# Low parts in two pieces, a later sums product, and a moved scaling in a float32 decoder kernel

## The chip, the cores and the metric

The kernel runs on one core of a Trainium2 chip. That core has TensorE for matrix products, VectorE and ScalarE for elementwise work, GpSimd (here it only issues DMAs), and SyncE, which issues most DMAs. The metric is the device time of one execution in microseconds. The profile names the engines PE (TensorE matmul), PEld (TensorE weight load), DVE (VectorE), ACT (ScalarE), POOL (GpSimd) and SP (SyncE). A line number such as L408 is a line of the kernel before the change.

## The reference

A decoder trunk of two layers works on one sequence of 512 tokens with 1024 features, all in float32. Each layer is half a SwiGLU FFN, a mixer, and half a second FFN, each behind an RMS norm. The first layer's mixer is a chunked gated linear attention (GLA), the second layer's a stick-breaking attention (SB). At the end stands one more RMS norm.

```python
def rmsnorm(x, g):
    xf = x.astype(jnp.float32)
    y = xf * lax.rsqrt(jnp.mean(xf * xf, axis=-1, keepdims=True) + EPS)
    return (y * g.astype(jnp.float32)).astype(x.dtype)

def swiglu(h, w_gate, w_up, w_down):
    return (jax.nn.silu(h @ w_gate) * (h @ w_up)) @ w_down
...
    for i in range(DEPTH):
        x = x + 0.5 * swiglu(rmsnorm(x, ffn1_norm[i]), ffn1_w_gate[i], ffn1_w_up[i], ffn1_w_down[i])
        h = rmsnorm(x, mix_norm[i])
        ...
        x = x + y.astype(x.dtype)
        x = x + 0.5 * swiglu(rmsnorm(x, ffn2_norm[i]), ffn2_w_gate[i], ffn2_w_up[i], ffn2_w_down[i])
    return rmsnorm(x, final_norm)
```

`w_gate` and `w_up` are 1024 x 2816, `w_down` is 2816 x 1024.

## The kernel before

**Number format.** Every operand of a product is cut into a high part (a cast to a reduced float32 on ScalarE, L148 for weights, tiles `wh`) and a low part (operand minus high part, a subtraction on VectorE, L150, tiles `wl`). A product of two operands is then three matmuls: high by high, low by high, high by low (`mm3`). Activations have the same two parts: `xh`/`xl` (not normed), `nh`/`nl` (normed), `hh`/`hl` (the FFN's inner values), `th`/`tl` (sums of normed halves).

**Phases.** Six phases follow one another: FFN, GLA, FFN, FFN, SB, FFN. The activations `xs` (eight tiles of 128 features by 512 tokens) stay on the chip. The weights stream in by DMA and are taken from one long list, `feed`; an entry is one or more weight tiles with a `body` that issues products and gives up control (`yield`) after pieces of them, so that other work can be put in between.

**An FFN phase.** Its first six entries work on activations that are not normed. Their results are multiplied by `R`, the inverse root of the mean square, when they leave the accumulator. `two_halves` runs the first two entries side by side: each has 24 matmuls and is driven in steps of six. In the three FFN phases after the first one (the third, fourth and sixth phase of all) a function is called in between: `sums_wide` adds up the squares over the features. ScalarE casts the sums to `sh` (L586), VectorE subtracts to `sl` (L588), and two matmuls with a matrix of ones go to the accumulator `ps_R`. `rstd_wide` makes `R` of it (L597 to L605, with a logarithm, an exponential and a square on ScalarE). Then `normed_input` (four pieces, L854 to L886) multiplies all eight `xs` by `R`, cuts them into `nh` and `nl`, and forms differences of their halves (`ts`). From the seventh entry on the products read `nh` and `nl`.

**Seven instead of eight products.** Larger blocks multiply two by two blocks with seven products and more additions (after Strassen and Winograd): `seven` for gate and up, `seven_down` for the down product of two of the six groups of inner features, two calls for each of those groups. So four FFNs have 16 `seven_down` in all. One `seven_down` consists of two entries with seven products of 12 matmuls (256 columns each) in this order: in `body_1` b11 (to accumulators `ws`, copied to `zs` by ScalarE), t1 (to `qs`), t2 (again to `ws`), b21 (to `zs`), and in `body_2` t3 (to `ws`), b22 (to `qs`), t4 (to `ws`). After each product `add` (L414, VectorE) takes the accumulator's content over into `xs`; the next product that goes to the same accumulator waits for that addition. `body_2` needs `s34`, two sums of weight blocks (VectorE, L399 and L400), cut into its parts by `split` at the end of the second step of `body_1`: the cast is ordered behind ScalarE's copies `v["copied"]`, the subtraction behind the last addition `added` of t1. Slice 0 to 1 of the parts is read by t3, slice 2 to 3 by b22.

**The end.** The last FFN ends token by token: `to_tokens` fetches the last norm's weights into `fin` (a DMA issued by GpSimd that gives all 128 partitions the same 1024 numbers), multiplies them by a constant on VectorE (L1617), and transposes `xs` on TensorE into `ps_T`, from which ScalarE copies them back (L1628). `back_tok` and `last` form the rest of the down product, the norm and the output.

**What sets the order.** A planner lays out each engine's instructions: it simulates the program with its own estimates and gives a free engine the ready instruction that stands first in the program. `tc.high_priority(n)` lets instructions count as n places earlier. `tc.issue_after(ins)`, also as `behind(ins)`, orders what is issued within it behind `ins`, for those instructions that run on the same engine as `ins`, without a wait for its end. Waits for data are put in by the framework, by the parts of a tile that are written and read. On the chip each engine runs its instructions strictly in the planned order.

Of the kernel before, what the change touches and what calls it, by code (L numbers as in the profile page):

```python
# [18 lines left out]
P = 128  # L19
T = 512  # L20
D = 1024
# [14 lines left out]
def flat(ps):  # L36

    return ps.rearrange("p (n two) -> p two n", two=2)
# [8 lines left out]
def decoder(ctx: ExitStack, tc: tile.TileContext, a: dict, out: bass.AP):  # L47
# [30 lines left out]

    def mm(ps, l, r, first, last):
        st["pe"] = nc.tensor.matmul(ps, l, r, start=first, stop=last).ins  # L80

    def mm3(ps, wh, wl, mh, ml, first, last):
        mm(ps, wh, turns(mh), first, False)
# [24 lines left out]
    def behind(ins):  # L108
        return tc.issue_after(ins) if ins is not None else ExitStack()

    class Entry:
# [13 lines left out]
                    self.views = [view(ch.load()) for ch, view, _, _ in self.units]  # L125
            return self.views

        def split(self, after=None, then=None):
            if self.W is None:
                self.W = []  # L130
                for r, (_, _, n, m) in zip(self.view(), self.units):
                    self.W.append(self.parts(r, n, m, after or self.casts_behind, then))

        def parts(self, r, n, m, after, then):
            few = n * m < 1024
            if few:

                h, l = (
                    st["few"].tile([P, n * m], F32R, tag="v" + t, bufs=1, name="w" + t) for t in "hl"
                )  # L140
            else:
                h, l = (wp.tile([P, n * m], F32R, tag="w" + t, bufs=4, name="w" + t) for t in "hl")
            h, l = (t.rearrange("p (n m) -> p n m", m=m) for t in (h, l))
            pieces = r if isinstance(r, tuple) else (r,)
            for i, part in enumerate(pieces):
                k = slice(i * n // len(pieces), (i + 1) * n // len(pieces))
                with behind(after):
                    nc.scalar.copy(h[:, k], part)  # L148
                with behind(then):
                    nc.vector.tensor_tensor(out=l[:, k], in0=part, in1=h[:, k].bitcast(F32), op=ALU.subtract)  # L150
            return h, l

    class Feed:
# [218 lines left out]
    def seven_down(pool, w, r0, hs, part):  # L372

        H = T // 2
        lower, upper = (
            Chunk(w[r0 : r0 + 4 * P, c : c + 256].rearrange("(f p) c -> p f c", p=P), 4, 256)
            for c in (part * 256, 512 + part * 256)
        )  # L380
        lower.few = upper.few = True
        v = {}

        def halves():

            lo, up = (c.load().rearrange("p (c two) d -> p two c d", two=2) for c in (lower, upper))
            return lo[:, 0], lo[:, 1], up[:, 0], up[:, 1]

        def sums_12(_):
            a11, _, a21, a22 = halves()  # L390
            s = v["s12"] = pool().tile([P, 4, 256], F32, tag="s", bufs=4, name="s12")
            nc.vector.tensor_tensor(out=s[:, 0:2], in0=a21, in1=a22, op=ALU.add)
            nc.vector.tensor_tensor(out=s[:, 2:4], in0=s[:, 0:2], in1=a11, op=ALU.subtract)
            return s

        def sums_34(_):
            a11, a12, a21, _ = halves()
            s = pool().tile([P, 4, 256], F32, tag="s", bufs=4, name="s34")
            nc.vector.tensor_tensor(out=s[:, 0:2], in0=a11, in1=a21, op=ALU.subtract)  # L399
            nc.vector.tensor_tensor(out=s[:, 2:4], in0=a12, in1=v["s12"][:, 2:4], op=ALU.subtract)  # L400
            return s

        def prod(ps, w, k0, m, b, first):
            for c in range(2):
                bh, bl = (turns(t) for t in hs[c][b])
                wh, wl = (t[:, k0 + c, m * P : (m + 1) * P] for t in w)
                for n, (l_, r_) in enumerate(((wh, bh), (wl, bh), (wh, bl))):
                    st["pe"] = nc.tensor.matmul(  # L408
                        ps, l_, r_, start=first and c + n == 0, stop=c == 1 and n == 2, skip_group_check=True
                    ).ins  # L410

        def add(m, up, col, ps):
            x = pair(xs[part * 2 + m + 4 * up][:, col * H : col * H + H])
            return nc.vector.scalar_tensor_tensor(out=x, in0=ps, scalar=0.5, in1=x, op0=ALU.mult, op1=ALU.add).ins  # L414

        def body_1(W):
            a11, s, v["a2"] = W
            ws, zs, qs = [], [], []
            for m in range(2):
                ws.append(psum("ps_w")[:, 0:H])  # L420
                prod(ws[m], a11, 0, m, "b11", True)
            for m in range(2):


                zs.append(psum("ps_z")[:, 0:H])
                with ahead():
                    v["copied"] = nc.scalar.copy(zs[m], ws[m]).ins
            yield

            ps = psum("ps_q")  # L430
            for m in range(2):
                qs.append(ps[:, m * H : (m + 1) * H])
                prod(qs[m], s, 0, m, "t1", m == 0)
            for m in range(2):
                added = add(m, 1, 1, flat(qs[m]))
            v["second"].split(v["copied"], added)
            yield
            for m in range(2):
                prod(ws[m], s, 2, m, "t2", False)
                add(m, 0, 1, flat(ws[m]))  # L440
            yield
            for m in range(2):
                prod(zs[m], v["a2"], 0, m, "b21", False)
                add(m, 0, 0, flat(zs[m]))
            v["w"], v["q"] = ws, qs
            yield

        def body_2(W):
            (s,) = W
            ws, qs = v["w"], v["q"]  # L450

            u3 = pool().tile([P, 2, H], F32, tag="c", bufs=1, name="u3")
            for m in range(2):
                prod(ws[m], s, 0, m, "t3", False)
                nc.scalar.copy(pair(u3[:, m]), flat(ws[m]))
                add(m, 1, 1, pair(u3[:, m]))
            yield
            for m in range(2):
                prod(qs[m], s, 2, m, "b22", False)
            for m in range(2):  # L460
                add(m, 0, 1, flat(qs[m]))
            yield
            for m in range(2):
                prod(ws[m], v["a2"], 2, m, "t4", False)
                add(m, 1, 0, flat(ws[m]))
            yield

        units = [(lower, lambda t: halves()[0], 2, 256), (lower, sums_12, 4, 256), (lower, lambda t: halves()[1::2], 4, 256)]
        feed.q.append(Entry(units, body_1))
        feed.q.append(Entry([(lower, sums_34, 4, 256)], body_2))  # L470
        v["second"] = feed.q[-1]
        feed.q[-1].v = v
# [106 lines left out]
        st["R"] = sp.tile([P, T], F32, tag="sq", name="R")  # L579
        nc.vector.tensor_copy(st["R"], ps)  # L580

    def sums_wide(pool):

        ss = st["ss"]
        h = sp.tile([P, T], F32R, tag="sq", name="sh")
        nc.scalar.copy(h, ss)  # L586
        l = pool.tile([P, T], F32R, tag="t", name="sl")
        nc.vector.tensor_tensor(out=l, in0=ss, in1=h.bitcast(F32), op=ALU.subtract)  # L588
        st["wide"] = ps = psum("ps_R")
        mm(ps, ones_r, turns(h), True, False)  # L590
        mm(ps, ones_r, turns(l), False, True)

    def rstd_wide():

# [12 lines left out]
    def two_halves(between=None):  # L607

        feed.finish()
        g = [feed.start(), feed.start()]  # L610
        for i in range(3):
            for x in g:
                next(x, None), next(x, None)
            if i == 0 and between is not None:
                between()

    def new_norm():
        st["h"], st["l"] = st["nh"], st["nl"]
# [16 lines left out]
    class FFN:  # L635
# [328 lines left out]
        def run(self, between=None):  # L964
            with tc.tile_pool(name="hp", bufs=8, reuse_waits="tile") as self.hp, tc.tile_pool(
# [4 lines left out]
                if st["ss"] is not None:  # L970
                    if self.after_ffn:
                        exp_ln_tables(st["closed"])
                    two_halves(lambda: sums_wide(self.tp))
                    rstd_wide()
                flush(self.defer)
                def spread(todo, n):
# [635 lines left out]
    def to_tokens(tp):  # L1612
        st["tp"] = tp
        fin = st["fin"] = tp.tile([P, D], F32, tag="s", bufs=4, name="fin")
        nc.gpsimd.dma_start(fin, a["final_norm"].partition_broadcast(P))

        nc.vector.tensor_scalar(out=fin, in0=fin, scalar1=2.0 * float(D) ** 0.5, scalar2=None, op0=ALU.mult)  # L1617

        for hf in range(2):
            ps = [psum("ps_T") for _ in range(NT)]  # L1620
            for m in range(4):
                for i in range(NT):
                    nc.tensor.transpose(
                        ps[i][:, m * P : (m + 1) * P], xs[hf * 4 + m][:, i * P : (i + 1) * P], ident
                    )
            for i in range(NT):
                xt[i, hf] = xs[hf * 4 + i]
                nc.scalar.copy(xt[i, hf], ps[i])  # L1628

    def last(dh, i, ps, c0, c1):  # L1630

# [335 lines left out]
```

## Time and profile before

| What | Value |
|---|---|
| median of 3 runs | 1772.12 us (1771.75 to 1773.25) |
| the profiled execution | 1772.11 us |
| its span in the trace | 1770.1 us |
| TensorE matmul busy | 1753.8 us (99%) |
| weight load busy | 1631.2 us (92%) |
| VectorE busy | 1505.5 us (85%) |
| ScalarE busy | 1062.8 us (60%) |
| moved from and to memory | 193.14 MB, mean 109 GB/s |

The profile lists for every instruction its start, its length, its engine, its line and its tiles (written as `out<-in`), and in brackets how long the engine stood idle before it and what ended that. Matmuls overlap: one lasts longer than the distance to the next, so the distance between two starts tells what a matmul costs in a full queue. `x2` on a row of the timeline means two instructions in direct succession, whose time is given together. The span runs from the first to the last instruction; the execution's time has some 2 us more around it.

### The profile page before, as it was taken

The numbers are of one execution on the slowest core, as the hardware profiler recorded it, in microseconds if no ns is written. First come the engines' busy times: TensorE is split into PE (matmuls) and PEld (weight loads), VectorE is DVE, ScalarE is ACT, GpSimd is POOL, SyncE is SP. The second block draws the span as 40 slices with busy tenths as digits, with TensorE's granted clock in tenths as the row PEclk, the third lists the DMA queues.
The fourth block names the chain that finished last, engine by engine and source line by source line (L and its number), as shares of the span: only waits on it lengthen the run. The fifth ranks groups of instructions, "written<-read, shape, count | busy, mean of one in ns | idle before, by whom it ended". The sixth has DMA issues, their size and how long they took to land.

```text
span 1770.1 us, 31362 instructions
## 1 busy us (share of the span) xinstructions
PE 1753.8 (99%) x12714; PEld 1631.2 (92%) x12714; DVE 1505.5 (85%) x2474; ACT 1062.8 (60%) x1883; POOL 55.6 (3%) x77
## 2 busy tenths in 40 slices
PE   9999999999999999999999999999999999999998
PEld 8999999889888999999889999999888889999997
DVE  8999797786888999888799988967898679997986
ACT  7556555554655556555556555655888745555555
POOL 0000000200000000000000000010000000000000
PEclk9999999999999999999999999999999999999999
DMA  5543434422123433444424334352212134434341
GB/s 168 154 124 104 137 104 147 113 72 73 49 94 97 131 108 120 119 120 127 136 89 132 108 119 137 100 130 84 84 49 76 68 96 131 131 103 130 107 130 63
DMA packets 186388, 193.14 MB, mean 109 GB/s; under 512 B 4930, under 2 KB 171124, under 8 KB 186244
## 3 DMA queue, kind: packets, MB, share of 16 engines
q1 hardware_dynamic: 177760, 175.91, 31.5%
q0 software_dynamic: 8240, 14.95, 4.6%
q8 instruction: 99, 1.62, 0.4%
q14 instruction: 45, 0.37, 0.1%
q10 hardware_dynamic: 244, 0.29, 0.0%
HBM read 175.17 MB, written 2.10 MB: 100 GB/s over the span
## 4 chain that ended last, share of the span: by engine, by line
PE 79%; DVE 11%; issue 5%; ACT 3%; DMA 1%; POOL 0%; DVEq 0%; SPq 0%; ACTq 0%; POOLq 0%
PE ps_w L755 19%; PE ps_f L80 14%; PE ps_d L80 14%; PE ps_q L755 9%; PE ps_t L80 4%; PE ps_z L755 4%; DVE wl L150 3%; PE ps_w L408 3%; PE ps_b L80 3%; PE ps_q L408 2%; PE ps_z L1455 1%; PE ps_oT L1540 1%; PE ps_bt L80 1%; PE ps_T L1525 1%; ACT wh L148 1%
## 5 line engine op out<-in xcount | busy, mean ns | idle before, releaser
L150 DVE TENSOR_TENSOR wl<-raw,wh 128x1024 fp32r<-128x1024 f32 x241 | 255.9, 1063 | 39.3 <-ACT wh L148 38.6
L150 DVE TENSOR_TENSOR wl<-s,wh 128x1024 fp32r<-128x1024 f32 x176 | 215.1, 1222 | 67.8 <-ACT wh L148 67.0
L148 ACT CAST wh<-raw 128x1024 fp32r<-128x1024 f32 x241 | 222.3, 923 | 67.8 <-PE ps_f L80 21.6
L755 PE MATMUL ps_w<-th,wl 128*128 128x256 f32 x864 | 237.7, 275 | 1.4 <-DVE wl L150 1.4
L755 PE MATMUL ps_w<-th,wh 128*128 128x256 f32 x864 | 239.0, 277 | 0.1
L755 PE MATMUL ps_w<-tl,wh 128*128 128x256 f32 x864 | 237.6, 275 | 0.0
L148 ACT CAST wh<-s 128x1024 fp32r<-128x1024 f32 x176 | 185.4, 1053 | 6.0 <-DVE s L741 6.0
L755 PEld LDWEIGHTS ps_w<-th,wl 128*128 128x128 f32 x864 | 165.8, 192 | 1.6 <-DVE wl L150 1.6
L755 PEld LDWEIGHTS ps_w<-th,wh 128*128 128x128 f32 x864 | 165.8, 192 | 0.9 <-ACT o L792 0.4
L80 PE MATMUL ps_f<-xh,wh 128*128 128x512 f32 x432 | 166.4, 386 | 0.0
L755 PEld LDWEIGHTS ps_w<-tl,wh 128*128 128x128 f32 x864 | 165.9, 192 | 0.0
L80 PE MATMUL ps_f<-xh,wl 128*128 128x512 f32 x432 | 164.2, 380 | 0.5 <-DVE wl L150 0.5
L80 PE MATMUL ps_f<-xl,wh 128*128 128x512 f32 x432 | 163.9, 379 | 0.0
L80 PE MATMUL ps_d<-hh,wh 128*128 128x512 f32 x416 | 157.8, 379 | 0.0
L80 PE MATMUL ps_d<-hh,wl 128*128 128x512 f32 x416 | 157.7, 379 | 0.0
L80 PE MATMUL ps_d<-hl,wh 128*128 128x512 f32 x416 | 157.7, 379 | 0.0
L150 DVE TENSOR_TENSOR wl<-rawd,wh 128x1024 fp32r<-128x1024 f32 (+1 forms) x100 | 95.1, 964 | 10.6 <-ACT wh L148 10.6
L783 ACT COPY ps_z<-ps_w 128x256 f32<-128x256 f32 x72 | 26.0, 361 | 121.2 <-PE ps_w L755 121.0
L359 POOL DMA_DIRECT2D x<-d x53 | 46.0, 911 | 1559.8 <-ACT d L358 1099.2
L80 PEld LDWEIGHTS ps_f<-xl,wh 128*128 128x128 f32 x432 | 81.6, 189 | 11.5
L80 PEld LDWEIGHTS ps_f<-xh,wl 128*128 128x128 f32 x432 | 81.7, 189 | 11.3 <-DVE wl L150 0.9
L80 PEld LDWEIGHTS ps_f<-xh,wh 128*128 128x128 f32 x432 | 81.7, 189 | 10.8
(355 smaller groups left out, 5393.1 us busy)
## 6 DMA issues: line engine op xcount, KB each, us to landing
raw<-in_ffn_w_gate_dram SPq DMA_DIRECT2D x43, 1024.0 KB, 5.4
raw<-in_ffn_w_up_dram SPq DMA_DIRECT2D x43, 1024.0 KB, 5.4
rawd<-in_ffn_w_down_dram SPq DMA_DIRECT2D x84, 512.0 KB, 4.0
x<-d POOLq DMA_DIRECT2D x53, 256.0 KB, 4.4
raw<-in_gla_w_in_dram SPq DMA_DIRECT2D x12, 1024.0 KB, 5.3
raw<-in_sb_w_in_dram SPq DMA_DIRECT2D x16, 512.0 KB, 3.7
raw<-in_gla_w_out_dram SPq DMA_DIRECT2D x4, 1024.0 KB, 5.1
raw<-in_sb_w_in_dram SPq DMA_DIRECT2D x4, 1024.0 KB, 5.1
```

The lines of the kernel that those rows point to most:

```text
L80: st["pe"] = nc.tensor.matmul(ps, l, r, start=first, stop=last).ins
L148: nc.scalar.copy(h[:, k], part)
L150: nc.vector.tensor_tensor(out=l[:, k], in0=part, in1=h[:, k].bitcast(F32), op=ALU.subtract)
L359: nc.gpsimd.dma_start(xs[k], d, accum_op=ALU.add)
L408: st["pe"] = nc.tensor.matmul(ps, l_, r_, start=first and c + n == 0, stop=c == 1 and n == 2, skip_group_check=True).ins
L755: st["pe"] = nc.tensor.matmul(o, l_, r_, start=first and j + n == 0, stop=j == 3 and n == 2, skip_group_check=True).ins
L783: v["copied"] = nc.scalar.copy(z, w).ins
L1455: nc.tensor.matmul(o_, l_, r_, start=first, stop=last, skip_group_check=True)
L1525: nc.tensor.transpose(ps[:, c0 : c0 + P], ys[yb][:, yc + j * P : yc + (j + 1) * P], ident)
L1540: nc.tensor.matmul(po[e * 64 : e * 64 + 64, j * P : T], self.v[j][:, c : c + 64], self.wt[p, e][bk][:, c0 : c0 + n], start=j == 0, stop=j ...
```

## The change

The change has three parts.

1. `s34` is no longer cut by `split`. `body_1` takes the two tiles itself and calls a new function, `low_34`. Its first call stands where `split` stood: it casts the two halves of `s34` in two instructions behind the same ScalarE copies and subtracts for the first half (slice 0 to 1) behind the last addition of t1. Its second call stands behind the two t2 additions and subtracts for the second half, ordered behind the last of them. `split` and `parts` lose their argument `then`.
2. `mm` notes every matmul in a list, `recent`. `two_halves` calls the function between no longer after both entries have done 12 matmuls each, but after the first of them has issued its other 12, and hands it the fourth last of these, which is the 33rd matmul of the two entries together. `sums_wide` orders its two matmuls behind that one, with a priority raised by 100.
3. The scaling of `fin` is issued behind the transposes and the copies, within `issue_after` of the last copy. The copy runs on ScalarE, the scaling on VectorE. The DMA of `fin` stays where it was.

```diff
     def mm(ps, l, r, first, last):
         st["pe"] = nc.tensor.matmul(ps, l, r, start=first, stop=last).ins
+        recent.append(st["pe"])
+
+    recent = []
...
                 with behind(after):
                     nc.scalar.copy(h[:, k], part)
-                with behind(then):
-                    nc.vector.tensor_tensor(out=l[:, k], in0=part, in1=h[:, k].bitcast(F32), op=ALU.subtract)
+                nc.vector.tensor_tensor(out=l[:, k], in0=part, in1=h[:, k].bitcast(F32), op=ALU.subtract)
...
         def sums_34(_):
             a11, a12, a21, _ = halves()
-            s = pool().tile([P, 4, 256], F32, tag="s", bufs=4, name="s34")
+            s = v["s34"] = pool().tile([P, 4, 256], F32, tag="s", bufs=4, name="s34")
...
+        def low_34(k0, added):
+
+            t, (h, l) = v["s34"], v["second"].W[0]
+            if k0 == 0:
+                v["cast"] = True
+                for k in (slice(0, 2), slice(2, 4)):
+                    with behind(v["copied"]):
+                        nc.scalar.copy(h[:, k], t[:, k])
+            k = slice(k0, k0 + 2)
+            with behind(added):
+                nc.vector.tensor_tensor(out=l[:, k], in0=t[:, k], in1=h[:, k].bitcast(F32), op=ALU.subtract)
+
...
             for m in range(2):
                 added = add(m, 1, 1, flat(qs[m]))
-            v["second"].split(v["copied"], added)
+            if v["second"].W is None:
+                v["second"].view()
+                v["second"].W = [tuple(wp.tile([P, 4, 256], F32R, tag="w" + t, bufs=4, name="w" + t) for t in "hl")]
+                low_34(0, added)
             yield
             for m in range(2):
                 prod(ws[m], s, 2, m, "t2", False)
-                add(m, 0, 1, flat(ws[m]))
+                added = add(m, 0, 1, flat(ws[m]))
+            if "cast" in v:
+                low_34(2, added)
             yield
...
-    def sums_wide(pool):
+    def sums_wide(pool, after):
...
         st["wide"] = ps = psum("ps_R")
-        mm(ps, ones_r, turns(h), True, False)
-        mm(ps, ones_r, turns(l), False, True)
+        with tc.high_priority(100), tc.issue_after(after):
+            mm(ps, ones_r, turns(h), True, False)
+            mm(ps, ones_r, turns(l), False, True)
...
         for i in range(3):
-            for x in g:
-                next(x, None), next(x, None)
-            if i == 0 and between is not None:
-                between()
+            for n, x in enumerate(g):
+                next(x, None)
+                next(x, None)
+                if between is not None and (i, n) == (1, 0):
+                    between(recent[-4])
...
-                    two_halves(lambda: sums_wide(self.tp))
+                    two_halves(lambda after: sums_wide(self.tp, after))
...
-        nc.vector.tensor_scalar(out=fin, in0=fin, scalar1=2.0 * float(D) ** 0.5, scalar2=None, op0=ALU.mult)
-
...
             for i in range(NT):
                 xt[i, hf] = xs[hf * 4 + i]
-                nc.scalar.copy(xt[i, hf], ps[i])
+                copied = nc.scalar.copy(xt[i, hf], ps[i]).ins
+
+        with tc.issue_after(copied):
+            nc.vector.tensor_scalar(out=fin, in0=fin, scalar1=2.0 * float(D) ** 0.5, scalar2=None, op0=ALU.mult)
```

More of the change, by code (lines that the diff above doesn't have):

```diff
@@ L126, in view, with split @@
             return self.views
-        def split(self, after=None, then=None):
+        def split(self, after=None):
             if self.W is None:
@@ L131, in split, with parts @@
                 for r, (_, _, n, m) in zip(self.view(), self.units):
-                    self.W.append(self.parts(r, n, m, after or self.casts_behind, then))
-        def parts(self, r, n, m, after, then):
+                    self.W.append(self.parts(r, n, m, after or self.casts_behind))
+        def parts(self, r, n, m, after):
             few = n * m < 1024
```

## The prediction

> **What bounds the kernel now.** I read the page's parts 1 and 2 first, then who waited for whom on TensorE, then the instructions of the code lines that the change touches, and last the timeline around each of those places.
>
> ```profile
> PE 1753.8 (99%) x12714; PEld 1631.2 (92%) x12714; DVE 1505.5 (85%) x2474; ACT 1062.8 (60%) x1883; POOL 55.6 (3%) x77
> ...
> PEclk9999999999999999999999999999999999999999
> ```
>
> TensorE is busy for 99% of the span at full granted clock. Nothing in the change takes a matmul away, so all it can win is idle TensorE time, and that is at most 1770.1 - 1753.8 = 16.3 us. Next comes where that idle time sits. The columns are engine, tile and line, whom it waited for, total us, times, longest.
>
> ```profile
> PE ps_R L80 <- ACT sh L586: 2.0, 3, 0.9
> PE ps_w L408 <- DVE x L414: 1.7, 8, 0.2
> PE ps_w L755 <- DVE wl L150: 1.4, 1, 1.4
> ```
>
> These are the three largest waits of TensorE, and each belongs to one part of the change: the product for the summed squares (L80, tile ps_R, three places), the first product of `body_2` in `seven_down` (L408), and one product late in the last FFN (L755), which I trace to `fin` below. The view counts only time in which no matmul was in flight. The distance between starts shows more, and I use that.
>
> **Part A: the second sums' low part in two pieces.**
>
> ```profile
> L408 PE MATMUL ps_w<-hh,wh x64: 275/275/275, 133.8 to 1702.1; 128*128 128x256 f32 x64
> ...
>   issue: 3.8, 12
> ```
>
> The t2 products are four of this kind per `seven_down`, so 64 of them make 16 executions. L408's weight loads stood still 12 times for 3.8 us. One of the 12:
>
> ```profile
> 677.18 0.75 DVE L414 SCALAR_TENSOR_TENSOR x<-ps_q,x 128x256 f32<-128x256 f32 x2
> 677.84 1.22 DVE L150 TENSOR_TENSOR wl<-s,wh 128x1024 fp32r<-128x1024 f32 x1
> 678.97 0.75 DVE L414 SCALAR_TENSOR_TENSOR x<-ps_w,x 128x256 f32<-128x256 f32 x2
> 679.64 0.75 DVE L414 SCALAR_TENSOR_TENSOR x<-ps_z,x 128x256 f32<-128x256 f32 x2
> 680.30 0.68 DVE L150 TENSOR_TENSOR wl<-raw,wh 128x512 fp32r<-128x512 f32 x1
> 680.90 1.22 DVE L150 TENSOR_TENSOR wl<-s,wh 128x1024 fp32r<-128x1024 f32 x1
> ...
> 677.27 0.61 ACT L148 CAST wh<-raw 128x512 fp32r<-128x512 f32 x1
> 677.79 1.04 ACT L148 CAST wh<-s 128x1024 fp32r<-128x1024 f32 x1
> ...
> 679.04 0.28 PE L408 MATMUL ps_z<-hl,wh 128*128 128x256 f32 x1
> 679.54 0.35 PE L408 MATMUL ps_w<-nh,wh 128*128 128x256 f32 x1 [0.22 <-DVE x L414]
> ...
> 680.95 0.28 PE L408 MATMUL ps_q<-hh,wh 128*128 128x256 f32 x1
> ```
>
> The low part (677.84) stands on VectorE ahead of the two t2 additions (678.97), and the first t3 product (679.54) writes the accumulator that the first of those additions reads. Products follow one another 0.11 us apart here, so it was due at 679.15 and came 0.39 us late. With half the low part there, VectorE is held 0.60 us (the distance from 680.30 to 680.90 for this shape) instead of 1.13 (677.84 to 678.97). The first t2 addition then starts at 678.44 and ends near 678.86. From the end of that addition today, about 679.39, to the product is 0.15 us, so t3 could start at 679.01, before it is due. The second piece follows the additions at about 679.1 and ends by 679.8; the product that reads it, the first b22 (today 680.95, then 680.56), has 0.7 us to spare. Each of the 12 stalls goes: **-3.8 us**.
>
> What it costs: per execution VectorE gains 2 x 0.60 - 1.13 = 0.07 us and ScalarE at most 2 x 0.61 - 1.04 = 0.18 us, since the cast is cut in two as well. The z additions and the next chunk's low parts (680.30, 680.90) move by that 0.07 us, and their readers come 2 us or more later, after the twelve products each of t3, b22 and t4 (12 x 0.11 us apiece). No DMA and no queue of SP or POOL is touched. Nothing is late next. At zero I put the four executions without a stall.
>
> [...]
>
> **Part B: the product for the summed squares behind nine more products.** Today the planner puts it after 29 products in the first and third place and after 24 in the second; now it is tied behind the 33rd, with its low half directly behind it.
>
> ```profile
> 553.75 0.38 PE L80 MATMUL ps_f<-xh,wh 128*128 128x512 f32 x1
> 559.79 0.38 PE L80 MATMUL ps_f<-xh,wl 128*128 128x512 f32 x1
> 560.76 0.48 PE L80 MATMUL ps_R<-sh,one_r 128*128 128x512 f32 x1 [0.59 <-ACT sh L586]
> 561.51 0.46 PE L80 MATMUL ps_R<-sl,one_r 128*128 128x512 f32 x1
> 561.81 0.38 PE L80 MATMUL ps_f<-xh,wl 128*128 128x512 f32 x1
> ...
> 560.74 0.69 DVE L588 TENSOR_TENSOR sl<-ss,sh 128x512 fp32r<-128x512 f32 x1 [0.68 <-ACT sh L586]
> ...
> 877.00 0.38 PE L80 MATMUL ps_f<-xh,wh 128*128 128x512 f32 x1
> 881.97 0.38 PE L80 MATMUL ps_f<-xl,wh 128*128 128x512 f32 x1
> 883.26 0.48 PE L80 MATMUL ps_R<-sh,one_r 128*128 128x512 f32 x1 [0.91 <-ACT sh L586]
> 883.99 0.48 PE L80 MATMUL ps_R<-sl,one_r 128*128 128x512 f32 x1
> 884.31 0.38 PE L80 MATMUL ps_f<-xh,wl 128*128 128x512 f32 x1
> ```
>
> A product takes 0.216 us (877.00 to 881.97 are 23 steps). First place: the 33rd starts at 560.66, the high half at 560.88 and finds its operand ready; the low half is due 0.32 us later at 561.20 but its operand is ready only at 561.43, so it starts at 561.51 as today. At 561.81 TensorE has done 33 products instead of 31: 2 x 0.216 = 0.43 us won. The third place is alike. Second place: high half at 884.13, low half at 884.45, the 34th product at 884.77; today the 26th starts at 884.31, so the 34th at 886.04: 1.27 us won, but the sums end 0.46 us later (884.45 against 883.99). So TensorE's own gain is 0.43 + 1.27 + 0.43 = 2.1 us.
>
> It does not all stay. The root of these sums starts a long stretch of VectorE work (`normed_input`) without a hole, and TensorE meets its end:
>
> ```profile
> core 0: us, DVE busy (x), PEclk, DMA share, GB/s
> 564.33:588.46 24.13, 24.09 (x43) 1.00 0.07 22
> 1444.67:1468.80 24.13, 24.10 (x43) 1.00 0.08 23
> ...
> 587.77 0.70 DVE L864 TENSOR_TENSOR nl<-xn,nh 128x512 fp32r<-128x512 f32 x1
> 588.57 0.43 PE L80 MATMUL ps_f<-nl,wh 128*128 128x512 f32 x1
> 588.84 0.38 PE L80 MATMUL ps_f<-nh,wh 128*128 128x512 f32 x1
> ...
> 910.60 1.30 DVE L864 TENSOR_TENSOR nl<-xn,nh 128x512 fp32r<-128x512 f32 x2
> 912.37 0.38 PE L80 MATMUL ps_f<-nl,wh 128*128 128x512 f32 x1
> ```
>
> At 588.57 TensorE reads the low part `nl` of the fourth normed input, which VectorE finished at 588.47: 0.1 us of slack, and the next start is already 0.05 us late. VectorE's 24.13 us before it are 24.09 busy. As the sums end when they end today, this chain stays where it is, and the 0.43 us are given back there, in the first and the third place. In the second place `nl` ends near 911.29 and is read at 912.37; TensorE would come at 911.10 and `nl` with its 0.08 us of handover at 911.83, so 0.54 us remain. **Part B: -0.5 us.** Its ends are -2.1 (the chain shortens too) and +0.5, the latter if a ScalarE cast of 1.04 us is planned into the root's chain in the second place, with `nl` handed over at 912.87 instead of 912.37. I take the value by rows of `nl`, which lie nearest to the cause.
>
> **Part C: the last norm's weights scaled behind the transposes.**
>
> ```profile
> 1718.44 0.70 DVE L1617 TENSOR_SCALAR fin<-fin 128x1024 f32<-128x1024 f32 x1 [4.27 <-DMA fin<-in_final_norm_dram]
> ...
> 1718.63 0.28 PE L755 MATMUL ps_w<-th,wh 128*128 128x256 f32 x1
> 1720.32 0.38 PE L755 MATMUL ps_w<-th,wl 128*128 128x256 f32 x1 [1.42 <-DVE wl L150]
> ```
>
> VectorE stood 4.27 us in front of this scaling, since its DMA had not landed, with low parts queued behind it, and TensorE lost 1720.32 - 1718.63 - 0.11 = 1.58 us. Really moved behind the transposes, the scaling (0.70 us) would run in VectorE's idle time and cost nothing. But the new order names a ScalarE copy, and `issue_after` orders only instructions of the named instruction's engine; the scaling is on VectorE. Its place in the program does move, but the trace shows that place does not hold it: it is written after every `wl` of that group and still ran ahead of them, because the planner found VectorE free and thought the DMA landed. No VectorE instruction stands between the old and the new place. I take **0**; the other end is -1.6 us.
>
> **Sum.** -3.8 - 0.5 + 0 = -4.3 us. The profiled execution took 1772.11 us (span 1770.1 and 2.0 around it), the median is 1772.12, so no correction is needed: **1767.8 us**. A difference of 0.2%, about what a measurement of this kernel can tell from no change, is 3.5 us: below 1768.6 is faster.
>
> **The rivals.**
> 1. Part C does move the scaling, because the planner's simulated order shifts. For it: one earlier free moment decides. Against: the missing tie. 1767.8 - 1.6 = 1766.2 us.
> 2. Part B keeps all its 2.1 us, because a low part of 1.1 us slips out of VectorE's full stretch into the holes before the root. 1767.8 - 1.6 = 1766.2 us as well. Against: the planner had those holes before.
> 3. The second instruction costs in full and on the path: 2 x 0.68 - 1.22 = 0.14 us, sixteen times 2.2 us, so 1770.0 us: no change. Against: 0.07 us in the full queue, behind work with slack. [...]
> 4. Slower: the planner puts another chunk's low part of 1.13 us between the first piece and the t2 additions. Its cast has been queued since 677.27 and is done at 677.88, before the first piece ends, so it could. It decides if the planner believes the t2 product unfinished at that point. The addition would start at 678.44 + 1.13 = 679.57 instead of 678.97, 0.60 us later in each of 16: 12 x 0.6 + 4 x 0.5 = 9.2 us, 1772.1 + 9.2 - 0.5 = 1780.8 us. Against: the additions come first in the program, and the t2 product that the first of them reads starts its last matmul before 677.5.
>
> **How the numbers follow.** Forecast 0.50, rival 1 0.17, rival 2 0.07, rival 3 0.15, rival 4 0.11. The likeliest's own range is 1767.2 (the 0.39 us of the quoted stall in all 12, 4.4 for 3.8) to 1768.8 (part B at its end of +0.5). The range over the cases reaches from 1764.5, where rivals 1 and 2 come together (-3.8 - 2.1 - 1.6 = -7.5), to 1772.0, which takes in rival 3 with half of part A's 3.8 us lost besides; it leaves out rival 4 and a small tail. Faster is 0.50 + 0.17 + 0.07 less the 0.06 of the forecast that lies above 1768.6: 0.68. Same is 0.15 + 0.06 = 0.21, slower 0.11.
>
> **What will show it.** Right: on VectorE two `wl` pieces of 128x512 from `s34` with the t2 additions between them, the stall line of the products' group (3.8 us, 12 times) near zero; TensorE's wait for `sh` gone, and instead a wait for `nl` of some 0.4 us in the first normed product of the third and the sixth phase; `fin` still at the head of a VectorE wait of about 4 us. Wrong: `fin` after the last ScalarE copy of `ps_T`; a `wl` of another chunk between the pieces; new TensorE waits for `wl` anywhere else, since the planner lays out the whole program anew.

## The result, and the profile after

The changed kernel takes 1767.22 us (median of 8 runs, 1766.55 to 1768.89) against 1772.13 us (8 runs) for the kernel before: a ratio of 0.9971, 95% interval 0.9962 to 0.9980. Beside the experiments, on another chip, it took 1766.66 us (9 runs) against 1771.17 (13 runs), a ratio of 0.9974 [0.9964, 0.9984]. The forecast was 1767.8.

| What | before | after |
|---|---|---|
| profiled execution, us | 1772.11 | 1767.14 |
| its span, us | 1770.1 | 1765.2 |
| TensorE matmul busy, us | 1753.8 | 1751.6 |
| VectorE busy, us (instructions) | 1505.5 (2474) | 1506.7 (2490) |
| ScalarE busy, us (instructions) | 1062.8 (1883) | 1063.3 (1899) |

The 16 new instructions on VectorE and on ScalarE are the second pieces. From the waits of TensorE in the profile after (tile and line, whom it waited for, total us, times, longest):

```profile
PE ps_w L776 <- DVE wl L152: 1.2, 1, 1.2
...
PE ps_f L80 <- DVE nl L885: 0.8, 3, 0.3
...
PE ps_R L80 <- DVE sl L607: 0.2, 1, 0.2
```

Of the three largest waits before, the 2.0 us for `sh` have shrunk to one of 0.2 us for `sl`, the 1.7 us for `x` in `seven_down` are gone, and the late product of the last FFN (now L776) still waits. New are three waits for `nl`.

The waits leave out what passes while a matmul is in flight, so I lined up all 12714 matmuls of the two traces, the n-th of one against the n-th of the other, and noted where the distance between their starts changes. Those steps show where the time went (a small drift between two places, at most some 0.1 us, is counted with the next place):

| Place | Step, us |
|---|---|
| first t3 product of twelve `seven_down` | 8 x -0.45 and 4 x -0.28, in all -4.7 |
| products of `seven` (L776) that write `ps_w` again, at 165, 708 and 1032 | +0.16, +0.21, +0.13 |
| sums, first place (561 to 589) | -0.77 + 0.66 + 0.49 = +0.38 |
| sums, second place (884 to 913) | -1.48 + 0.54 = -0.94 |
| sums, third place (1441 to 1470) | -0.75 + 0.31 + 0.49 = +0.05 |
| the product late behind `fin` | -0.26 |

The last matmul of the changed kernel starts 4.95 us earlier than that of the kernel before, and the span fell by 4.9. Now the same places in the timeline that the prediction showed of before.

Part A, the `seven_down` at 677 us (VectorE, then TensorE):

```profile
676.53 0.74 DVE L416 SCALAR_TENSOR_TENSOR x<-ps_q,x 128x256 f32<-128x256 f32 x2
677.19 0.67 DVE L428 TENSOR_TENSOR wl<-s,wh 128x512 fp32r<-128x512 f32 x1
677.79 0.74 DVE L416 SCALAR_TENSOR_TENSOR x<-ps_w,x 128x256 f32<-128x256 f32 x2
678.46 0.67 DVE L428 TENSOR_TENSOR wl<-s,wh 128x512 fp32r<-128x512 f32 x1
679.06 0.74 DVE L416 SCALAR_TENSOR_TENSOR x<-ps_z,x 128x256 f32<-128x256 f32 x2
...
678.40 0.28 PE L410 MATMUL ps_z<-hl,wh 128*128 128x256 f32 x1
678.52 0.28 PE L410 MATMUL ps_w<-nh,wh 128*128 128x256 f32 x1
678.63 0.28 PE L410 MATMUL ps_w<-nh,wl 128*128 128x256 f32 x1
```

One piece (677.19), the t2 additions, the other piece (678.46): nothing of another chunk between them. The first t3 product (678.52) follows its neighbour after 0.12 us, without a bracket; before, it came 0.50 us after its neighbour.

Part B, the first place (TensorE, ScalarE, VectorE, then TensorE 27 us later):

```profile
559.71 0.38 PE L80 MATMUL ps_f<-xl,wh 128*128 128x512 f32 x1
560.06 0.48 PE L80 MATMUL ps_R<-sh,one_r 128*128 128x512 f32 x1
560.79 0.48 PE L80 MATMUL ps_R<-sl,one_r 128*128 128x512 f32 x1 [0.24 <-DVE sl L607]
561.11 0.38 PE L80 MATMUL ps_f<-xh,wh 128*128 128x512 f32 x1
...
561.95 1.05 ACT L151 CAST wh<-raw 128x1024 fp32r<-128x1024 f32 x1 [1.94 <-PE ps_f L80]
562.90 0.63 ACT L653 ACTIVATE R<-v 128x512 f32<-128x512 f32 x1
...
561.31 0.69 DVE L617 TENSOR_SCALAR v<-ps_R 128x512 f32<-128x512 f32 x1 [0.57 <-PE ps_R L80]
...
587.24 0.38 PE L80 MATMUL ps_f<-nh,wl 128*128 128x512 f32 x1
587.87 0.48 PE L80 MATMUL ps_f<-nl,wh 128*128 128x512 f32 x1 [0.25 <-DVE nl L885]
```

The low half still waits for `sl`, as forecast, and 27 us on TensorE waits for `nl`: 587.87 - 587.24 - 0.22 = 0.41 us late. One thing is new. A weight cast of 1.05 us now stands on ScalarE ahead of the logarithm that begins the root, and is itself released only by a TensorE product; `v` was done at 562.00 and the logarithm began at 562.90. Before, such a cast stood between the logarithm and the exponential in the first and third place and outside the chain in the second; now it stands ahead of the logarithm in all three. The second place, first before (VectorE), then after (ScalarE, then VectorE):

```profile
884.51 0.69 DVE L597 TENSOR_SCALAR v<-ps_R 128x512 f32<-128x512 f32 x1 [0.57 <-PE ps_R L80]
887.19 0.69 DVE L604 SCALAR_TENSOR_TENSOR v<-ps_R,v 128x512 f32<-128x512 f32 x1 [1.99 <-ACT ps_R L603]
```

```profile
883.79 1.05 ACT L151 CAST wh<-raw 128x1024 fp32r<-128x1024 f32 x1 [2.41 <-PE ps_f L80]
884.74 0.62 ACT L653 ACTIVATE R<-v 128x512 f32<-128x512 f32 x1
...
883.14 0.69 DVE L617 TENSOR_SCALAR v<-ps_R 128x512 f32<-128x512 f32 x1 [1.03 <-PE ps_R L80]
884.87 1.23 DVE L152 TENSOR_TENSOR wl<-raw,wh 128x1024 fp32r<-128x1024 f32 x1 [1.04 <-ACT wh L151]
886.69 0.69 DVE L624 SCALAR_TENSOR_TENSOR v<-ps_R,v 128x512 f32<-128x512 f32 x1 [0.60 <-ACT ps_R L623]
```

The cast holds up the root there as well: from `v` to VectorE's next step of the root it is 3.55 us instead of 2.68. Its low part (884.87) uses VectorE's hole while VectorE waits for the root; it then no longer stands in the full stretch behind it.

Part C, the end (VectorE, then TensorE):

```profile
1713.49 0.69 DVE L1649 TENSOR_SCALAR fin<-fin 128x1024 f32<-128x1024 f32 x1 [4.02 <-DMA fin<-in_final_norm_dram]
...
1713.93 0.28 PE L776 MATMUL ps_w<-th,wh 128*128 128x256 f32 x1
1715.37 0.38 PE L776 MATMUL ps_w<-th,wl 128*128 128x256 f32 x1 [1.16 <-DVE wl L152]
```

The scaling is where it was, ahead of the low parts, and VectorE still stands 4.02 us before it, although the cast that the low part at 1714.10 reads was done at 1711.43 (it starts at 1710.38 and takes 1.05 us). The stop is 1715.37 - 1713.93 - 0.11 = 1.33 us where it was 1.58: the DMA of `fin` took 7.1 us to land, not 7.4. The kernel with part B alone, which lacks part C, shows the same thing larger: there the DMA landed after 6.8 us, and the step at this place is -0.61 us.

### The profile page after: what moved, and what is told of

It reads as the page before. It is cut to its first block, busy times and chain, and to the rows that moved or that the text cites. A ratio compares the mean times of both kernels' runs of the same rounds, so it can differ in the third digit from the quotient of the medians.

```text
span 1765.2 us, 31380 instructions
## 1 busy us (share of the span) xinstructions
PE 1751.6 (99%) x12714; PEld 1630.2 (92%) x12714; DVE 1506.7 (85%) x2490; ACT 1063.3 (60%) x1899; POOL 55.7 (3%) x77
## 4 chain that ended last, share of the span: by engine, by line
PE 86%; DVE 9%; ACT 3%; issue 1%; DMA 1%; SPq 0%; DVEq 0%; ACTq 0%
PE ps_w L776 22%; PE ps_d L80 15%; PE ps_q L776 11%; PE ps_f L80 10%; PE ps_z L776 5%; PE ps_w L410 5%; PE ps_t L80 4%; PE ps_b L80 3%; PE ps_q L410 2%; DVE wl L152 1%; PE ps_z L410 1%; PE ps_z L1476 1%; PE ps_oT L1561 1%; DVE xn L878 1%; PE ps_bt L80 1%
## 5 line engine op out<-in xcount | busy, mean ns | idle before, releaser
L152 DVE TENSOR_TENSOR wl<-s,wh 128x1024 fp32r<-128x1024 f32 x160 | 195.2, 1220 | 64.5 <-ACT wh L151 64.0
L776 PE MATMUL ps_w<-th,wh 128*128 128x256 f32 x864 | 239.0, 277 | 0.2
L776 PE MATMUL ps_w<-th,wl 128*128 128x256 f32 x864 | 237.7, 275 | 1.2 <-DVE wl L152 1.2
L776 PE MATMUL ps_w<-tl,wh 128*128 128x256 f32 x864 | 237.6, 275 | 0.0
L151 ACT CAST wh<-s 128x1024 fp32r<-128x1024 f32 x160 | 168.6, 1054 | 6.0 <-DVE s L762 6.0
L776 PEld LDWEIGHTS ps_w<-th,wh 128*128 128x128 f32 x864 | 165.8, 192 | 1.4 <-ACT o L813 1.1
L776 PEld LDWEIGHTS ps_w<-th,wl 128*128 128x128 f32 x864 | 165.8, 192 | 1.4 <-DVE wl L152 1.4
L776 PEld LDWEIGHTS ps_w<-tl,wh 128*128 128x128 f32 x864 | 165.9, 192 | 0.0
```

Source lines behind the costliest of these rows:

```text
L776: st["pe"] = nc.tensor.matmul(o, l_, r_, start=first and j + n == 0, stop=j == 3 and n == 2, skip_group_check=True).ins
```

## The experiments

Kernels were run on three chips, each beside the kernel before (1771.26 us, 19 runs, for the parts alone, the later place of the sums and the scaling really moved; 1771.0, 13 runs, for the cut, the order and the kernel with GpSimd; 1771.17, 13 runs, for both together). So each is told by its ratio to the kernel before on the same chip. Edits are against the changed kernel unless it is said otherwise.

### Parts alone

Part A without B and C, and part B without A and C, each put into the kernel before.

> Part A alone, on the kernel before. Theory (the three parts add up as the trace of the changed kernel shows them, A -4.2, B -0.5, C a quarter of a microsecond that is only the DMA's own scatter): 1772.1 - 4.2 = 1767.9 us, the twelve stalls ahead of t3 gone, the waits for sh as before (0.59, 0.91 and 0.5 us idle). Rival (A's gain comes about only because B shifts the planner's order): 1771 us or more.

> Part B alone, on the kernel before. Theory (TensorE wins 2.1 us at the sums and gives most of it back at the low part nl, which waits for VectorE's full stretch behind the root): 1772.1 - 0.5 = 1771.6 us, with new waits for nl of 0.4 us in all three places and the twelve stalls ahead of t3 still there. Rival (the gain at the sums stays): 1770.0 us and no wait for nl.

Part A alone: 1767.14 us (9 runs), ratio 0.9976 [0.9967, 0.9986], 4.1 us less. Part B alone: 1770.51 us, ratio 0.9995 [0.9986, 1.0003], 0.75 us less, an interval that holds no change. From TensorE's waits with A alone, and then with B alone:

```profile
PE ps_R L80 <- ACT sh L605: 1.5, 3, 0.6
PE ps_w L774 <- DVE wl L152: 1.4, 1, 1.4
```

```profile
PE ps_w L411 <- DVE x L417: 1.6, 8, 0.2
...
PE ps_w L772 <- DVE wl L153: 0.8, 1, 0.8
PE ps_f L80 <- DVE nl L881: 0.8, 3, 0.3
```

With A alone no wait for `x` or `nl` is left; with B alone the waits for `x` stay and those for `nl` appear. So `nl` belongs to B. B's steps in this trace are -0.90 + 0.31 + 0.49, -1.53 + 0.54 and -0.80 + 0.30 + 0.49: TensorE wins 3.23 us at the sums and hands back 0.61 at once (the wait for `sl`, in the first and third place) and 1.52 at `nl`. Rival 2 (all 2.1 us stay) falls. With A alone, the twelve steps are there again (-4.7 in all); beside them stand 0.4 us more in the first 8 us and 0.5 us less wait for `sh` in the second place, where A touches nothing. The +0.2 us at 165 and 708 is missing, as it is in the second trace of the changed kernel: so it is taken as scatter of one execution, not as a cost of part A. The +0.13 us at 1032 is there again with A alone (+0.12) and in the second trace of the changed kernel (+0.11), but not in the kernel with both edits below; whether part A causes it stays open.

### What in part A wins: the cut or the order

The order without the cut: the casts stay in two instructions, the whole low part stands behind the t2 additions.

```diff
-            k = slice(k0, k0 + 2)
+            if added is None:
+                return
+            k = slice(0, 4)
...
-                low_34(0, added)
+                low_34(0, None)
```

> The changed kernel with the whole low part of s34 in one VectorE instruction behind the t2 additions. It tells the new order from the cut in two. Theory (both are needed: the additions free the accumulator, and t3 reads the first half of the low part): t3 now waits for the whole low part, which ends about 1.0 us after t3 is due in twelve executions and about 0.3 us in the other four, so 1767.2 + 13 = 1780 us. Rival (the order alone makes the gain): 1767.2 us.

The cut without the order: both pieces stand ahead of the t2 additions.

```diff
                 low_34(0, added)
+                low_34(2, added)
             yield
...
-            if "cast" in v:
-                low_34(2, added)
```

> The changed kernel with both pieces of the low part ahead of the t2 additions. It shows the cut in two without the new order, and what the cut itself costs. Theory (t3 waits for the addition, not for the low part, and two pieces take VectorE 0.07 us longer than one): the twelve stalls are back at 0.39 + 0.07 us, 1767.2 + 4.2 + 0.8 = 1772.2 us. Rival (t3 can start as soon as its own half of the low part is there): 1767.2 us.

Both kernels hold parts B and C. The order alone is slower: 1782.14 us (4 runs), ratio 1.0061 [1.0046, 1.0076]. The cut alone is back at the start: 1771.78 us (10 runs), ratio 1.0004 [0.9994, 1.0013]. TensorE's largest wait in each, and one place of each in the timeline, first of the order alone, then of the cut alone:

```profile
PE ps_w L410 <- DVE wl L430: 8.3, 11, 0.8
...
683.61 0.38 PE L410 MATMUL ps_w<-nh,wl 128*128 128x256 f32 x1 [0.76 <-DVE wl L430]
```

```profile
PE ps_w L410 <- DVE x L416: 2.2, 8, 0.3
...
678.05 1.28 DVE L428 TENSOR_TENSOR wl<-s,wh 128x512 fp32r<-128x512 f32 x2
679.25 0.75 DVE L416 SCALAR_TENSOR_TENSOR x<-ps_w,x 128x256 f32<-128x256 f32 x2
```

Behind the additions the whole low part is too late for t3's second product, which reads its first half. Against the changed kernel this costs 15.6 us of TensorE at t3, where 13 was expected: some 1.1 us in eight of the sixteen, 1.7 in three and 0.35 in five. Ahead of them, two pieces hold VectorE 679.25 - 678.05 = 1.20 us instead of 1.13, and the old wait grows from 1.7 to 2.2 us. So the second instruction does cost something where it stands in front of the path: lined up with the kernel before, t3 comes 0.05 to 0.07 us later still in the twelve that stalled and 0.03 us in the other four, 0.85 us in all. That is the 0.07 us per cut that was expected. The time is back at the start and not above it because part B wins 0.9 us in this trace. What wins is one piece on each side of the additions.

### A later place for the sums

```diff
-                    between(recent[-4])
+                    between(recent[-1])
```

This ties the product behind the 36th product instead of the 33rd: 0.65 us later, by which time `sl` should be ready.

> The changed kernel with the sums product tied behind the 36th product instead of the 33rd. Rival (each product that goes ahead delays the sums, so the root and with it nl come later by up to 3 x 0.216 us): the root 0.1, 0.64 and 0.42 us later in the three places, 1767.2 + 1.2 = 1768.4 us. Theory (in the changed kernel the root does not wait for the sums but for ScalarE's cast of the next weights, which stands ahead of the logarithm and waits for the first entry's last product; with that product ahead of the sums the cast starts about 1.2, 0.4 and 0.8 us earlier): the root 0.8, 0.1 and 0.5 us earlier, less waiting for nl, 1767.2 - 1.4 = 1765.8 us.

1764.74 us, ratio 0.9965 [0.9952, 0.9977]: 6.5 us less than before, where the changed kernel wins 4.5 to 4.9. No wait for `nl` is long enough to stand in the list of waits. The first place (TensorE, ScalarE, then TensorE later):

```profile
560.92 0.38 PE L80 MATMUL ps_R<-sh,one_r 128*128 128x512 f32 x1
561.13 0.38 PE L80 MATMUL ps_R<-sl,one_r 128*128 128x512 f32 x1
...
561.12 1.05 ACT L151 CAST wh<-raw 128x1024 fp32r<-128x1024 f32 x1 [0.92 <-PE ps_f L80]
562.27 0.63 ACT L653 ACTIVATE R<-v 128x512 f32<-128x512 f32 x1
...
587.25 0.48 PE L80 MATMUL ps_f<-nl,wh 128*128 128x512 f32 x1
```

Both halves now pass 0.21 us apart and without a stop. And although the sums are asked for later, the root comes earlier: the weight cast ahead of the logarithm is released by the end of the 36th product (560.70 + 0.38 = 561.08), which no longer stands behind the two halves. It starts at 561.12 instead of 561.95, though this trace runs 0.4 us later up to there, the logarithm 0.63 us earlier (562.27 instead of 562.90), and `nl` is read at 587.25 instead of 587.87. Lined up with the changed kernel, the steps are -0.76 and -0.22 in the first place, -0.13 in the second, -0.50 and -0.22 in the third. Of the first, 0.35 us is only that the sums were late in that trace of the changed kernel. Against its second trace the steps are -0.39 and -0.22 in the first and the third place and -0.13 in the second, 1.35 us in all, where 1.4 was expected. So the chain is not tied to the end of the sums alone, as I had it, but to that cast as well.

### The scaling really moved

```diff
-                nc.vector.tensor_tensor(out=l[:, k], in0=part, in1=h[:, k].bitcast(F32), op=ALU.subtract)
+                st["lowest"] = nc.vector.tensor_tensor(out=l[:, k], in0=part, in1=h[:, k].bitcast(F32), op=ALU.subtract).ins
...
-        with tc.issue_after(copied):
+        with tc.issue_after(st["lowest"]):
```

Now the instruction named is one of VectorE, the last low part written before the scaling.

> The changed kernel with the scaling of fin ordered behind the last low part of the last weights, an instruction of VectorE itself, instead of behind a ScalarE copy. Theory (part C did not move the scaling, because its tie names another engine): the scaling now runs in VectorE's idle time at about 1741, the wait for the DMA and TensorE's stop of 1.33 us go, 1767.2 - 1.3 = 1765.9 us. Rival (the low parts behind it have another wait in the same place): 1767.2 us.

1764.77 us, ratio 0.9964 [0.9951, 0.9978]. TensorE, ScalarE, GpSimd and SyncE have the same order as in the changed kernel; on VectorE only the scaling has moved. From its line's listing and the timeline of TensorE:

```profile
L1649 DVE TENSOR_SCALAR fin<-fin x1: 690/690/690, 1734.1 to 1734.1; 128x1024 f32<-128x1024 f32 x1
...
1713.37 0.28 PE L776 MATMUL ps_w<-th,wh 128*128 128x256 f32 x1
1713.48 0.28 PE L776 MATMUL ps_w<-th,wl 128*128 128x256 f32 x1
```

The scaling runs at 1734.1 us with no wait before it, and no one waits for it. The product with `wl` follows after 0.11 us. The step against the changed kernel is -1.43 us at this place (-1.57 against its second trace). It is the only step of 0.4 us or more, and the change of the tie accounts for it: in the changed kernel, part C moved nothing.

### Both together

The last two edits in one kernel, and on the same chip the changed kernel once more.

> The changed kernel itself once more, so that the next one stands beside it on the same chip. Expected by every theory: 0.9971 of the kernel before, within its interval of 0.9962 to 0.998.

> The changed kernel with both edits that gained: the scaling of fin tied to a VectorE instruction and the sums product behind the 36th product. Theory (they act in different places, so they add): 1.4 and 1.2 us by the two traces, so 2.6 us less than the changed kernel, a ratio to the kernel before of 0.9956. Rival (the later stages take one of them back): no more than 1.4 us less, 0.9963.

1763.72 us (5 runs), ratio 0.9960 [0.9947, 0.9972], against 1766.66 us and 0.9974 for the changed kernel: 2.9 us less, so the two gains add up. It is the fastest kernel of this study. The two largest waits of TensorE that are left in it are one for `gT`, 0.9 us, and two for `e`, 0.6 us together; neither is touched by the change.

### VectorE's full stretch relieved by GpSimd

`nl` is bound by VectorE's full stretch in `normed_input`. Here the differences `ts` of that stretch go to GpSimd, which has no work there (0.00 us in each of the three stretches before).

```diff
             def sub(o, p, q):
-                nc.vector.tensor_tensor(out=o, in0=p, in1=q, op=ALU.subtract)
+                nc.gpsimd.tensor_tensor(out=o, in0=p, in1=q, op=ALU.subtract)
```

> The changed kernel with the sixteen subtractions per phase that form the sums ts of the normed input's halves on GpSimd instead of VectorE (0.34 us each there). Theory (nl is late only because VectorE is full from the root to it): the three waits for nl of 0.41 us go, 1767.2 - 1.2 = 1766.0 us. Rival (GpSimd slows VectorE or is itself too slow for the products of the sums): 1767.2 us or more, with waits of TensorE for tl or th.

1787.46 us (4 runs), ratio 1.0085 [1.007, 1.010]: much slower. From the groups of instructions of VectorE between 560 and 600 us (shapes, count, then busy us and mean ns of one), first of the changed kernel:

```profile
L885 DVE TENSOR_TENSOR nl<-xn,nh 128x512 fp32r<-128x512 f32 x8 | 5.4, 683 | 0.0
...
L885 DVE TENSOR_TENSOR hl<-t,hh 128x512 fp32r<-128x512 f32 x4 | 2.7, 684 | 0.0
```

and then with the differences on GpSimd, with some rows of the timeline (VectorE, then GpSimd):

```profile
L885 DVE TENSOR_TENSOR nl<-xn,nh 128x512 fp32r<-128x512 f32 x8 | 8.9, 1147 | 0.0
...
L885 DVE TENSOR_TENSOR hl<-t,hh 128x512 fp32r<-128x512 f32 x2 | 2.4, 1216 | 0.0
...
576.21 1.23 DVE L933 TENSOR_TENSOR t<-t 128x512 f32<-128x512 f32 x1
577.36 2.36 DVE L885 TENSOR_TENSOR nl<-xn,nh 128x512 fp32r<-128x512 f32 x2
579.64 1.21 DVE L885 TENSOR_TENSOR hl<-t,hh 128x512 fp32r<-128x512 f32 x1
...
586.64 0.68 DVE L931 TENSOR_TENSOR t<-ps_f,R 128x512 f32<-128x512 f32 x1
...
576.97 1.06 POOL L894 TENSOR_TENSOR ts<-xn,ts 128x256 f32<-128x256 f32 x1
577.99 1.18 POOL L894 TENSOR_TENSOR ts<-xn 128x256 f32<-128x256 f32 x1
579.13 1.18 POOL L894 TENSOR_TENSOR ts<-xn,ts 128x256 f32<-128x256 f32 x1
...
586.14 1.18 POOL L894 TENSOR_TENSOR ts<-xn,ts 128x256 f32<-128x256 f32 x1
```

VectorE's low-part subtractions (L885), which read no accumulator, take 1.15 to 1.22 us on the mean instead of 0.68. The instruction at 586.64, which reads an accumulator, stays at 0.68, although GpSimd is at work at the same time (586.14). The stretch got longer: TensorE's waits for `nl` rose from 0.8 to 7.1 us, and new waits for `nh` come to 4.4 us. Waits for tl or th, which the rival named, are not in the list. The experiment did not relieve the stretch, so what `nl` would give back if it were shorter was not measured this way; the later place of the sums measured it from the other end.

## Why the prediction was right

**Part A** was forecast at -3.8 us and is -4.7 by the steps in the profile after; alone it measured -4.1 us. Its mechanism held in every row: the first t2 addition was forecast at 678.44 instead of 678.97, 0.53 us earlier, and follows the t1 additions after 677.79 - 676.53 = 1.26 us instead of 678.97 - 677.18 = 1.79 us, which is 0.53 us; no other low part came in between, and the stall of t3 is gone in all twelve. The term that was too small is the price of a stall. I took the 3.8 us that the group's line gives as idle time of the weight loads. The distance of the starts is larger: 0.39 us at the stalled product and some 0.06 at the one after it, 0.45 us in eight of the twelve, and 0.28 us in the other four. I had this number and put it into the low end only, and there with a slip: 12 x 0.39 is 4.7, not 4.4.

**Part B** was forecast at -0.5 us and sums to -0.51 in the profile after, but not for the reasons given place by place. In the first and third place I forecast 0.43 won and 0.43 given back. The second trace of the changed kernel and part B alone have that to about 0.1 us (-0.07 and +0.01; -0.11 and 0). The +0.38 of the first place in the profile after is not in them: there a weight cast that waits 3.35 us for its DMA, at 547 us, came later than the work around it, the sums and all up to the root were 0.3 us late, and TensorE waited longer for `sl` (+0.66 instead of +0.31). That link to the DMA is read from one trace and not tested.

In the second place I forecast -1.27 + 0.73 = -0.54, and it is -1.48 + 0.54 = -0.94. At the sums a term was mis-sized: I gave each half of the product 0.32 us, the distance from rows where it had stood still, and in a full queue it takes 0.21 or 0.22 (the rows of the experiment behind the 36th product), 0.2 us for the two. What the place nets goes by `nl`, which came some 0.46 us earlier than forecast. Three things make that up. The sums end 0.21 us earlier, by the shorter product. The case that I had as part B's upper end came true, the cast in the root's chain, and adds 3.55 - 2.68 = 0.87 us. But at the same time its low part left the full stretch, which I had as rival 2's reason: from the root's next step to the end of `nl` it is 909.66 - 886.69 = 22.97 us instead of 911.29 - 887.19 = 24.10, which is 1.13 us less. The last two had been weighed alone, not as two consequences of one cast.

So B is nearer to -1.0 us than to -0.5 by two of three traces (-0.07 - 0.94 + 0.01 in the second one of the changed kernel), and one execution's scatter brought the sum to the forecast.

**Part C** was forecast at 0 and moved nothing. The -0.26 us is the landing of the DMA. The reason given, that the tie names an instruction of another engine, is borne out by the experiment: with a tie to an instruction of VectorE the scaling moved, and no other instruction changed its place in the order.

**The rivals.** Rival 1 (the scaling moves anyway) is refuted by the row of `fin` after; the price that I gave it, 1.6 us, was 1.4 to 1.6 in the experiment. Rival 2 is refuted by the waits for `nl`. Rival 3 (the second instruction costs in full) is half right: with both pieces ahead of the additions the cut does show, 0.07 us of VectorE each time, of which TensorE loses 0.05 to 0.07 at each of the twelve stalls, but in the order of the change it is hidden, and VectorE's whole work rose by only 1.2 us. The 0.14 us per cut that it took as the full price is there in the busy time of single instructions, 2 x 0.68 (the mean of the 32 pieces) against 1.22, and not in the distance in the queue, 0.07 us. Rival 4 (another chunk's low part between the pieces) did not occur at any of the sixteen.

## What to carry to other kernels

When an instruction on a busy engine stands ahead of one that frees a buffer, cut it by what its readers need first, and put that other instruction between the pieces; the cut alone and the order alone won nothing here. Price a stall by the distance between starts before and at it, not by the idle time that a list of waits shows. And after moving work with an ordering tie, look in the profile whether it moved: a tie to an instruction of another engine did nothing, and the tie to an instruction of the same engine was worth another 1.4 to 1.6 us.

## What the runs showed that I had not expected

VectorE got slower beside GpSimd, but not in every instruction. While GpSimd ran its differences of 128x256, which took 1.06 to 1.18 us in the rows shown (the shortest of all 64 took 0.73), VectorE's 128x512 subtractions took 1.15 to 1.22 us on the mean instead of 0.68. They started 1.14 us apart (577.36 to 579.64 for two) instead of 0.60, in turn with GpSimd's (577.99, 579.13). The instruction at 586.64, with one operand in an accumulator, took 0.68 us beside GpSimd. What makes the two kinds differ, the runs do not show.

And asking for a result later can bring it earlier: with the sums' product three products further back, the root began 0.63 us earlier, because the product had delayed the TensorE work that released a cast standing ahead of the root on ScalarE.
